# Batched matrix product in float32: loading y in 24 KB runs, transposing x on VectorE, and four 32-row tiles on TensorE

## The chip, the cores and the metric

One core of one Trainium2 chip (the experiments below ran on four chips in all, so runs are compared by their ratio to the kernel before). The metric is the device time of one execution in microseconds (us), as the median of several executions. The span of a profile is about 1.8 us shorter than the time of the same execution. A difference is called a class (faster, slower) only above 2%.

## The reference

```python
batch, dim_i, dim_j, dim_k = 32, 256, 512, 384
x: (batch, dim_i, dim_j) float32      # 16.8 MB
y: (batch, dim_j, dim_k) float32      # 25.2 MB
out = einsum('bij,bjk->bik', x, y)    # 12.6 MB, float32
```

In both kernels the matmuls take x and y with the contracted j on the partitions. y is loaded that way. x is loaded with i there, and both kernels transpose it so that j is. Both kernels multiply in float16 and accumulate in float32.

## The kernel before

The unit of work is two batches. x is loaded for four batches in one DMA, 32 partitions a batch, so each partition receives one run of 16384 B. y is loaded one batch per DMA with j spread over 128 partitions: four rows a partition, runs of 6144 B.

```python
def load_x(q):
    x_of[q] = x_pool.tile([P, R, J], F32, name="x_sb")
    keep(nc.sync.dma_start(out=x_of[q],
         in_=x[q * Q : (q + 1) * Q].rearrange("g (p r) j -> (g p) r j", r=R)))
# load(u), cut:
    y_of[u] = y_pool.tile([P, G, NJ, K], F32, name="y_sb")
    for g in range(G):
        keep(nc.sync.dma_start(out=y_of[u][:, g],
             in_=y[u * G + g].rearrange("(q t) k -> q t k", q=P)))
```

x is transposed by TensorE against an identity, in float32 into PSUM, and cast to float16 on the way out by VectorE and ScalarE in turn (128 x 512 at a time, 32 on either engine). Those two engines also cast y. A matmul contracts over 128 rows and has 64 output columns; two of them share a PSUM tile.

```python
# multiply(u), cut:
    o_ps = opsum_pool.tile([P, K], F32, name="o_ps")
    for t in range(NJ):
        for g in range(G):
            a = (u * G + g) % Q
            keep(nc.tensor.matmul(o_ps[g * M : (g + 1) * M],
                 xt_sb[:, t, e, a * PQ : (a + 1) * PQ].rearrange("c p h -> c (p h)"),
                 y_r[:, g, t], start=(t == 0), stop=(t == NJ - 1)))
```

One DMA queue carries everything. A unit's store is issued two steps after its y is cast.

## Time and profile before

| | before |
|---|---|
| median time | 136.04 us |
| span of the profile | 134.3 us |

The prediction below shows the page's main rows and what they mean. Two views that it does not show matter later. The first is the page's row of the instruction queue (queue, kind, packets, MB, share of 16 engines): packets of kind "instruction", which the page counts on the same 16 DMA engines as the data.

```profile
q8 instruction: 6, 0.10, 0.3%
```

The second is the table of stretches (stretch, us, busy us of PE, PEld, DVE, ACT and POOL with instruction counts, clock, DMA share, GB/s).

```profile
104.00:126.00 22.00, 17.58 (x156) 14.21 (x153) 11.19 (x26) 12.41 (x26) 0.00 (x0) 0.89 1.01 420
126.00:130.00 4.00, 2.40 (x30) 1.76 (x26) 1.52 (x3) 1.01 (x3) 0.00 (x0) 1.00 0.95 392
130.00:134.30 4.30, 0.00 (x0) 0.00 (x0) 0.00 (x0) 0.00 (x0) 0.00 (x0) 0.81 0.51 209
```

The last but one number is the DMA share: full until 126 us, 0.95 until 130, then the tail.

Each DMA here is spread over 16 DMA engines, and the trace records when each of them landed its part. I call the time from the first to the last of the 16 the **spread**. It is 0.6 us for the first load (landed from 8.0 to 8.6 us), 1.8 us from about 47 us on, and 2.0 us near 126 us. So some engines run behind the others, and the work that needs a DMA starts after the latest of them: the first transposes of x, for which all 16 parts had landed at 8.59, started at 8.72 us. (The records do not name the engine: "the latest" is the last of a DMA's 16 landings.)

### The profile page before, as it was taken

What the parts mean: (1) busy time and instruction counts of PE and PEld (TensorE: products, weight loads), DVE (VectorE), ACT (ScalarE), POOL (GpSimd) and SP (SyncE); (2) the same over time, 40 slices, a digit from 0 to 9 for tenths busy, and PEclk for the clock granted to TensorE, in tenths of its full rate; (3) what the DMA queues carried; (4) which work ended last, traced back from release to release, by engine and by line L of the source; (5) the groups of instructions that cost most, each with busy time, mean ns of one, the idle gap of its engine ahead of it and who ended that gap; (6) DMA issues with size and microseconds to landing.
All of it is one profiled execution on the core that took longest, in us unless ns stands there. A gap on an engine that the chain in (4) does not pass through costs nothing.

```text
span 134.3 us, 1968 instructions
## 1 busy us (share of the span) xinstructions
PE 88.5 (66%) x768; PEld 73.2 (55%) x768; DVE 56.2 (42%) x128; ACT 63.9 (48%) x129; POOL 0.7 (1%) x6
## 2 busy tenths in 40 slices
PE   0049494979299767786099771976439986597920
PEld 0049474768177666666078661864427665476810
DVE  0004717471743365711634318460363425628620
ACT  3004837662762476712744428560475336738610
POOL 2000000000000000000000000000000000000000
PEclk9999999999959999999968999999965899779997
DMA  5999999999999999999999999999999999999993
GB/s 112 415 400 450 409 417 421 456 388 421 417 448 408 409 428 421 457 394 417 413 443 436 408 417 428 442 422 402 425 423 444 426 402 427 419 427 419 417 394 158
DMA packets 8073, 54.65 MB, mean 407 GB/s; under 512 B 896, under 2 KB 896, under 8 KB 7040
## 3 DMA queue, kind: packets, MB, share of 16 engines
q1 hardware_dynamic: 8064, 54.53, 97.8%
q8 instruction: 6, 0.10, 0.3%
q14 instruction: 3, 0.02, 0.0%
HBM read 41.94 MB, written 12.58 MB: 406 GB/s over the span
## 4 chain that ended last, share of the span: by engine, by line
DMA 78%; PE 13%; ACT 4%; DVE 0%; issue 0%
DMA y_sb<-in_y_dram 40%; DMA x_sb<-in_x_dram 38%; PE o_ps L130 9%; PE t_ps L99 3%; ACT xt_sb L107 2%; ACT y_r L116 1%; ACT o_sb L143 1%; DVE o_sb L145 0%
## 5 line engine op out<-in xcount | busy, mean ns | idle before, releaser
L130 PE MATMUL o_ps<-y_r,xt_sb 128*64 128x384 f16 x512 | 52.4, 364 | 28.5 <-ACT o_sb L143 20.8
L130 PEld LDWEIGHTS <-xt_sb 128*64 128x64 f16 x512 | 39.1, 121 | 38.8 <-issue 22.4
L116 ACT CAST y_r<-y_sb 128x384 f16<-128x384 f32 x64 | 29.5, 514 | 38.7 <-DMA y_sb<-in_y_dram 38.6
L99 PE MATMUL t_ps<-identity,x_sb 128*128 128x128 f32 x256 | 36.9, 301 | 11.4 <-DMA x_sb<-in_x_dram 11.4
L99 PEld LDWEIGHTS t_ps<-identity,x_sb 128*128 128x128 f32 x256 | 34.1, 211 | 16.0 <-issue 16.0
L118 DVE CAST y_r<-y_sb 128x384 f16<-128x384 f32 x64 | 20.0, 356 | 46.7 <-DMA y_sb<-in_y_dram 46.7
L107 ACT CAST xt_sb<-t_ps 128x512 f16<-128x512 f32 x32 | 22.4, 731 | 23.6 <-PE t_ps L99 23.6
L105 DVE CAST xt_sb<-t_ps 128x512 f16<-128x512 f32 x32 | 22.6, 728 | 24.1 <-PE t_ps L99 23.8
L145 DVE COPY o_sb<-o_ps 128x384 f32<-128x384 f32 x32 | 16.3, 544 | 2.1 <-PE o_ps L130 2.1
L143 ACT COPY o_sb<-o_ps 128x384 f32<-128x384 f32 x32 | 13.9, 492 | 1.3 <-PE o_ps L130 1.3
L107 ACT ACT_TABLE_LOAD x1 | 1.3, 1283 | 0.7 <-PEq L192 0.7
masks.py:199 POOL TENSOR_SCALAR_AFFINE_SELECT identity<-identity 128x128 f32<-128x128 f32 x1 | 0.3, 294 | 0.1
masks.py:197 POOL MEMSET identity<- 128x128 f32 x1 | 0.2, 206 | 0.3 <-POOLq L192 0.3
L192 POOL MEMSET const-bfloat16-1.0<- 128x1 bf16 x1 | 0.1, 102 | 0.0
L192 POOL MEMSET const-uint8-127<- 128x1 uint8 x1 | 0.1, 102 | 0.0
L192 POOL MEMSET const-float32-0.0<- 128x1 f32 x1 | 0.1, 99 | 0.2 <-issue 0.2
L192 POOL MEMSET const-float32-1.0<- 128x1 f32 x1 | 0.1, 99 | 0.0
## 6 DMA issues: line engine op xcount, KB each, us to landing
y_sb<-in_y_dram SPq DMA_DIRECT2D x32, 768.0 KB, 17.9
x_sb<-in_x_dram SPq DMA_DIRECT2D x8, 2048.0 KB, 20.8
out_dram<-o_sb SPq DMA_DIRECT2D x16, 768.0 KB, 17.8
```

Of the source, the lines that this page charges most:

```text
L99: nc.tensor.transpose(t_ps[:, f, h], x_sb[:, h * NE + e + f, t::NJ], identity)
L105: keep(nc.vector.tensor_copy(dst, t_ps))
L107: keep(nc.scalar.copy(dst, t_ps))
L116: keep(nc.scalar.copy(yr_of[u][:, g, t], y_sb[:, g, t]))
L118: keep(nc.vector.tensor_copy(yr_of[u][:, g, t], y_sb[:, g, t]))
L130: nc.tensor.matmul(o_ps[g * M : (g + 1) * M], xt_sb[:, t, e, a * PQ : (a + 1) * PQ].rearrange("c p h -> c (p h)"), y_r[:, g, t], start=(t ...
L143: keep(nc.scalar.copy(o_of[u][:, e], ps_of[u][e]))
L145: keep(nc.vector.tensor_copy(o_of[u][:, e], ps_of[u][e]))
L192: nc = _bacc.Bacc("TRN2", target_bir_lowering=False, num_devices=1)
```

## The change

The intent: fewer and longer DMA packets for y, no transposes on TensorE (and no casts on ScalarE), four small matmuls at once. The unit becomes a group of four batches, 32 partitions a batch for both x and y, so a partition's y run is 24576 B. x is cast to float16 and its 4-byte words (pairs of float16) are transposed in 32 x 32 blocks by VectorE. Matmuls contract over 32 rows with 128 output columns, and a group fills all eight buffers of the PSUM pool ("banks" in the prediction). ScalarE copies them out in blocks of 64 partitions, VectorE half of those of the last group. Stores are issued a group's load later (DEFER = 3).

```diff
-Q = 4; G = 2; LAG = 4
+Q = 4; WIDE = 32; NARROW = 64; DEFER = 3
...
+    def load(n):                       # x as before, then y:
+        y_of[n] = y_pool.tile([P, T, K], F32, name="y_sb")
+        src = y[n * Q : (n + 1) * Q].rearrange("g (q t) k -> (g q) t k", t=T)
+        parts = 4 if n == N - 1 else 1
+        for a in range(parts): ...     # one DMA for each part
...
+    def transpose_x(n):
+        x_r = xr_pool.tile([P, R, J], MM_DT, name="x_r")
+        keep(nc.vector.tensor_copy(x_r, x_of.pop(n)))                    # L83
+        words = x_r.bitcast(F32)
+        src = words.rearrange("p (b h e) (q t) -> p b e t h q", b=2, e=NE, t=TW)
+        dst = xt_of[n].rearrange("p e t (h s b) -> p b e t h s", s=PQ, b=2)
+        for e in range(NE):
+            for b in range(2):
+                keep(nc.vector.transpose(dst[:, b, e], src[:, b, e]))    # L96
...
+    def multiply(n):                   # for each of 4 pieces a of y:
+            keep(nc.vector.tensor_copy(y_r[:, a : a + step], y_sb[:, a : a + step]))  # L107
+            for e in range(NE):
+                for t in range(a, a + step):
+                    for g in range(Q):
+                        s = slice(g * PQ, (g + 1) * PQ)
+                        keep(nc.tensor.matmul(ps_of[n][e][g],            # L113
+                             xt[s, e, t // 2, :, t % 2], y_r[s, t],
+                             start=(t == 0), stop=(t == T - 1)))
...
+    for n in range(2):
+        load(n)
+    for n in range(N):
+        transpose_x(n)
+        multiply(n)
+        collect(n)                     # copies: L139 ScalarE, L137 VectorE
+        if n + 2 < N:
+            load(n + 2)
+        if n + 2 - DEFER >= 0 and n + 2 < N:
+            store(n + 2 - DEFER)
+    for n in range(N - DEFER, N):
+        store(n)
```

(Lines reflowed and cut; all of the old load, transpose, round_y, multiply, collect and store is removed. `pieces(n)` is 4 and `width(n)` is NARROW for every group.)

More of the change, by code (lines that the diff above doesn't have):

```diff
@@ L15 @@
 Q = 4
-G = 2
-LAG = 4
+WIDE = 32
+NARROW = 64
+DEFER = 3
 @with_exitstack
@@ L32 @@
     _, _, K = y.shape
-    M = P // G
-    NE = I // M
-    NJ = J // P
     PQ = P // Q
     R = I // PQ
-    H = R // NE
-    U = B // G
-    const_pool = ctx.enter_context(tc.tile_pool(name="const", bufs=1))
-    x_pool = ctx.enter_context(tc.tile_pool(name="x_pool", bufs=3))
-    y_pool = ctx.enter_context(tc.tile_pool(name="y_pool", bufs=5))
+    T = J // PQ
+    TW = T // 2
+    NE = I // P
+    N = B // Q
+    x_pool = ctx.enter_context(tc.tile_pool(name="x_pool", bufs=2))
+    y_pool = ctx.enter_context(tc.tile_pool(name="y_pool", bufs=2))
@@ L49 @@
+    xr_pool = ctx.enter_context(tc.tile_pool(name="xr_pool", bufs=1))
+    xt_pool = ctx.enter_context(tc.tile_pool(name="xt_pool", bufs=2))
     yr_pool = ctx.enter_context(tc.tile_pool(name="yr_pool", bufs=2))
-    xt_pool = ctx.enter_context(tc.tile_pool(name="xt_pool", bufs=2))
-    o_pool = ctx.enter_context(tc.tile_pool(name="o_pool", bufs=5))
-    tpsum_pool = ctx.enter_context(tc.tile_pool(name="tpsum", bufs=4, space=bass.MemoryType.PSUM))
-    opsum_pool = ctx.enter_context(tc.tile_pool(name="opsum", bufs=4, space=bass.MemoryType.PSUM))
+    o_pool = ctx.enter_context(tc.tile_pool(name="o_pool", bufs=DEFER + 2))
@@ L56, with width, pieces @@
+    psum_pool = ctx.enter_context(
+        tc.tile_pool(name="psum", bufs=2 * Q, space=bass.MemoryType.PSUM)
+    )
     keep = tc.keep_in_program_order
-    identity = const_pool.tile([P, P], F32)
-    make_identity(nc, identity)
-    x_of, y_of, yr_of, xt_of, ps_of, o_of = {}, {}, {}, {}, {}, {}
-    def load_x(q):
-        x_of[q] = x_pool.tile([P, R, J], F32, name="x_sb")
+    x_of, y_of, xt_of, yr_of, ps_of, o_of = {}, {}, {}, {}, {}, {}
+    def width(n):
+        return NARROW
+    def pieces(n):
+        return 4
@@ L65, in load_x @@
+    def load(n):
+        x_of[n] = x_pool.tile([P, R, J], F32, name="x_sb")
         keep(
             nc.sync.dma_start(
-                out=x_of[q],
-                in_=x[q * Q : (q + 1) * Q].rearrange("g (p r) j -> (g p) r j", r=R),
-            )
-        )
-    def load(u):
-        if u == 0:
-            load_x(0)
-        if (u + 1) * G % Q == 0 and u + 1 < U:
-            load_x((u + 1) * G // Q)
-        y_of[u] = y_pool.tile([P, G, NJ, K], F32, name="y_sb")
-        for g in range(G):
+                out=x_of[n],
+                in_=x[n * Q : (n + 1) * Q].rearrange("g (p r) j -> (g p) r j", r=R),
+            )
+        )
+        y_of[n] = y_pool.tile([P, T, K], F32, name="y_sb")
+        src = y[n * Q : (n + 1) * Q].rearrange("g (q t) k -> (g q) t k", t=T)
+        parts = 4 if n == N - 1 else 1
+        for a in range(parts):
+            s = slice(a * T // parts, (a + 1) * T // parts)
+            keep(nc.sync.dma_start(out=y_of[n][:, s], in_=src[:, s]))
@@ new lines, in transpose_x @@
+    def transpose_x(n):
+        x_r = xr_pool.tile([P, R, J], MM_DT, name="x_r")
+        keep(nc.vector.tensor_copy(x_r, x_of.pop(n)))
+        xt_of[n] = xt_pool.tile([P, NE, TW, P], F32, name="xt_sb")
+        words = x_r.bitcast(F32)
+        if width(n) == WIDE:
+            src = words.rearrange("p (h e) (q t) -> p e t h q", e=NE, t=TW)
+            dst = xt_of[n].rearrange("p e t (h s) -> p e t h s", s=PQ)
+            for e in range(NE):
+                keep(nc.vector.transpose(dst[:, e], src[:, e]))
+        else:
+            src = words.rearrange("p (b h e) (q t) -> p b e t h q", b=2, e=NE, t=TW)
[3 more added lines that the diff above has]
+                    keep(nc.vector.transpose(dst[:, b, e], src[:, b, e]))
@@ new lines, in multiply @@
+    def multiply(n):
+        xt = xt_of.pop(n).bitcast(MM_DT).rearrange("p e t (m c) -> p e t m c", c=2)
+        y_sb = y_of.pop(n)
+        y_r = yr_pool.tile([P, T, K], MM_DT, name="y_r")
+        ps_of[n] = [
+            [psum_pool.tile([P, K], F32, name="o_ps") for _ in range(Q)] for _ in range(NE)
+        ]
+        step = T // pieces(n)
+        for a in range(0, T, step):
+            keep(nc.vector.tensor_copy(y_r[:, a : a + step], y_sb[:, a : a + step]))
+            for e in range(NE):
+                for t in range(a, a + step):
+                    for g in range(Q):
+                        s = slice(g * PQ, (g + 1) * PQ)
+                        keep(
+                            nc.tensor.matmul(
+                                ps_of[n][e][g],
+                                xt[s, e, t // 2, :, t % 2],
+                                y_r[s, t],
+                                start=(t == 0),
+                                stop=(t == T - 1),
+                            )
+                        )
@@ new lines, in collect @@
+    def collect(n):
+        w = width(n)
+        per = P // w
+        o_of[n] = o_pool.tile([P, R, K], F32, name="o_sb")
+        o = o_of[n].rearrange("p (u f) k -> p u f k", u=Q // per)
+        for u in range(Q // per):
+            for e in range(NE):
+                for v in range(per):
+                    g = u * per + v
+                    ps = ps_of[n][e][g]
+                    on_vector = n == N - 1 and g % 2 == 1
+                    for h in range(per):
+                        src = ps[h * w : (h + 1) * w]
+                        dst = o[v * w : (v + 1) * w, u, h * NE + e]
+                        if on_vector:
+                            keep(nc.vector.tensor_copy(dst, src))
+                        else:
+                            keep(nc.scalar.copy(dst, src))
+        del ps_of[n]
@@ L80, in load, with store @@
+    def store(n):
+        w = width(n)
+        per = P // w
+        o = o_of.pop(n).rearrange("p (u f) k -> p u f k", u=Q // per)
+        for u in range(Q // per):
+            b = n * Q + u * per
             keep(
                 nc.sync.dma_start(
-                    out=y_of[u][:, g],
-                    in_=y[u * G + g].rearrange("(q t) k -> q t k", q=P),
-                )
-            )
-    def transpose(q, half):
-        x_sb = x_of[q]
-        if half == 0:
-            xt_of[q] = xt_pool.tile([P, NJ, NE, Q * PQ, H], MM_DT, name="xt_sb")
-        n = 0
-        for t in range(half * NJ // 2, (half + 1) * NJ // 2):
-            for e in range(0, NE, 2):
-                t_ps = tpsum_pool.tile([P, 2, H, Q * PQ], F32, name="t_ps")
-                for f in range(2):
-                    for h in range(H):
-                        keep(
-                            nc.tensor.transpose(
-                                t_ps[:, f, h], x_sb[:, h * NE + e + f, t::NJ], identity
-                            )
-                        )
-                dst = xt_of[q][:, t, e : e + 2].rearrange("c f p h -> c f h p")
-                if n % 2 == 0:
-                    keep(nc.vector.tensor_copy(dst, t_ps))
-                else:
-                    keep(nc.scalar.copy(dst, t_ps))
-                n += 1
@@ L110, in round_y @@
-    def round_y(u):
-        y_sb = y_of.pop(u)
-        yr_of[u] = yr_pool.tile([P, G, NJ, K], MM_DT, name="y_r")
-        for g in range(G):
-            for t in range(NJ):
-                if t % 2 == 0:
-                    keep(nc.scalar.copy(yr_of[u][:, g, t], y_sb[:, g, t]))
-                else:
-                    keep(nc.vector.tensor_copy(yr_of[u][:, g, t], y_sb[:, g, t]))
-    def multiply(u):
-        xt_sb, y_r = xt_of[u * G // Q], yr_of.pop(u)
-        ps_of[u] = []
-        for e in range(NE):
-            o_ps = opsum_pool.tile([P, K], F32, name="o_ps")
-            ps_of[u].append(o_ps)
-            for t in range(NJ):
-                for g in range(G):
-                    a = (u * G + g) % Q
-                    keep(
-                        nc.tensor.matmul(
-                            o_ps[g * M : (g + 1) * M],
-                            xt_sb[:, t, e, a * PQ : (a + 1) * PQ].rearrange("c p h -> c (p h)"),
-                            y_r[:, g, t],
-                            start=(t == 0),
-                            stop=(t == NJ - 1),
-                        )
-                    )
@@ L139, in collect @@
-    def collect(u):
-        o_of[u] = o_pool.tile([P, NE, K], F32, name="o_sb")
-        for e in range(NE):
-            if e % 2 == 0:
-                keep(nc.scalar.copy(o_of[u][:, e], ps_of[u][e]))
-            else:
-                keep(nc.vector.tensor_copy(o_of[u][:, e], ps_of[u][e]))
-        del ps_of[u]
-    def store(u):
-        keep(
-            nc.sync.dma_start(
-                out=out[u * G : (u + 1) * G].rearrange("g (m e) k -> (g m) e k", e=NE),
-                in_=o_of.pop(u),
-            )
-        )
@@ L157 @@
-    ahead = LAG - 2
-    for u in range(ahead):
-        load(u)
-    for s in range(U + 2):
-        if s + ahead < U:
-            load(s + ahead)
-        if s == 0:
-            transpose(0, 0)
-            transpose(0, 1)
-        if s >= 2:
-            collect(s - 2)
-        if 1 <= s <= U:
-            multiply(s - 1)
-        if s < U:
-            round_y(s)
-        for half in range(2):
-            q = (s + 1 - half) * G // Q
-            if (s + 1 - half) * G % Q == 0 and 0 < q < B // Q:
-                transpose(q, half)
-        if s >= 2:
-            store(s - 2)
+                    out=out[b : b + per].rearrange("g (s f) k -> (g s) f k", s=w),
@@ L181 @@
+                    in_=o[:, u],
+                )
+            )
+    for n in range(2):
[10 more added lines that the diff above has]
+        store(n)
 _INS = ['x', 'y']
```

## The prediction

> **What bounds the kernel now.** I read the page from the top: busy shares, the 40 slices, the DMA queue, the chain that ended last, then the groups of instructions. After that I read the timeline of TensorE and of the last 30 us, and the trace's records of single DMA packets. First the page.
>
> ```profile
> span 134.3 us, 1968 instructions
> PE 88.5 (66%) x768; PEld 73.2 (55%) x768; DVE 56.2 (42%) x128; ACT 63.9 (48%) x129; POOL 0.7 (1%) x6
> ...
> PEclk9999999999959999999968999999965899779997
> DMA  5999999999999999999999999999999999999993
> ...
> DMA packets 8073, 54.65 MB, mean 407 GB/s; under 512 B 896, under 2 KB 896, under 8 KB 7040
> ...
> q1 hardware_dynamic: 8064, 54.53, 97.8%
> ...
> DMA 78%; PE 13%; ACT 4%; DVE 0%; issue 0%
> ```
>
> No compute engine passes 66%. The DMA row is at 9 from the second slice to the last but one, the queue's packets fill 97.8% of 16 engines' time, and the chain is 78% DMA. So the kernel is bound by the time its DMA packets take. The packet records split that time: 1024 packets of 16384 B (x, one per partition and load), median 611 ns; 6144 of 6144 B (4096 of y, 2048 of the output), median 234 ns, mean 235.8; 896 semaphore writes of 9 ns (56 DMAs x 16 engines). Per engine that is 40.3 + 90.6 + 0.5 = 131.4 us. The data packets run from 1.78 to 132.93 us, so there is almost no hole. The x sum holds about 1.1 us of slow first packets (26 of them over 700 ns, up to 1996). The only hole worth a name is at the end: in the last 4 us the engines lose about 1 us, part of it because the last store is issued at 129.1 us, after the last copy out of PSUM. The span ends 1.3 us after the last packet, and the timed median is 136.04 - 134.3 = 1.8 us over the profiled span.
>
> Next, the engines that the change reworks, in the table of groups and two pieces of TensorE's timeline (start, length, what):
>
> ```profile
> L130 PE MATMUL o_ps<-y_r,xt_sb 128*64 128x384 f16 x512 | 52.4, 364 | 28.5 <-ACT o_sb L143 20.8
> ...
> L99 PE MATMUL t_ps<-identity,x_sb 128*128 128x128 f32 x256 | 36.9, 301 | 11.4 <-DMA x_sb<-in_x_dram 11.4
> ...
> L118 DVE CAST y_r<-y_sb 128x384 f16<-128x384 f32 x64 | 20.0, 356 | 46.7 <-DMA y_sb<-in_y_dram 46.7
> ...
> L143 ACT COPY o_sb<-o_ps 128x384 f32<-128x384 f32 x32 | 13.9, 492 | 1.3 <-PE o_ps L130 1.3
> ```
>
> ```profile
> 107.94 2.79 PE L130 MATMUL o_ps<-y_r,xt_sb 128*64 128x384 f16 x32 [0.87 <-ACT xt_sb L107]
> ...
> 115.54 4.47 PE L130 MATMUL o_ps<-y_r,xt_sb 128*64 128x384 f16 x32 [2.69 <-ACT o_sb L143]
> ```
>
> In the first burst 32 matmuls start (2.79 - 0.33) / 31 = 79.5 ns apart, where one takes 326 ns from start to end: two column tiles run at once, 159 ns each. The second burst is the same work after an idle stretch of 2.69 us, and takes 1.7 us longer: that is the PEclk row's 5s, a clock record of 3.4 us at half rate. Two ScalarE copies in a row take 0.87 us in the timeline, so one costs 0.39 us more behind another (0.48 alone).
>
> [...]
>
> **The change part by part.**
>
> DMA. x and the output keep their runs (16384 and 6144 B). y goes from 4096 packets of 6144 B to 7 groups of 128 partitions at 24576 B = 896, and the last group in four parts, 512 of 6144 B. From the two medians a packet costs (611 - 234) / (16384 - 6144) = 0.0368 ns a byte and 8 ns fixed, so 24576 B take 913 ns, with the usual excess 915. That such a run stays one packet is my assumption; all shorter ones do. Per engine: x 40.3; y 896 x 0.915 / 16 = 51.2 and 512 x 0.2358 / 16 = 7.5; output 2048 x 0.2358 / 16 = 30.2; semaphores 35 DMAs x 0.009 = 0.3. Sum 129.6, against 131.4: **1.8 us less**. If the last stores are ready in time, up to 0.3 us of the hole at the end goes too.
>
> TensorE loses the 256 fp32 transposes (36.9 us) and has 1024 matmuls of 32 rows x 128 columns in place of 512: if four row tiles run at once, 159 / 4 = 40 ns apart, 128 x 0.040 = 5.1 us a group of four batches. I use 40 to 55 ns, as the weight loads of 128 columns may not all hide, and add 1.7 us for the clock: 6.8 to 8.7 us.
>
> VectorE per group: [...] Sum 8.4 (11) us of the roughly 16 us that a group's DMA takes (8 packets per engine of x, 8 of y, 16 of output: 4.9 + 7.3 + 3.8). It lies beside the transfers.
>
> ScalarE loses all casts (51.9 us) and takes all copies out of PSUM but half of the last group's: 16 a group of 64 partitions. The free size is unchanged, so I take the same 0.39 to 0.43 us: 6.3 to 6.9 us a group.
>
> What is new is a loop. One group fills all 8 PSUM banks, so the next group's first matmuls must wait until the twelfth of the 16 copies has freed the fourth bank. Copies of the first half of the banks start some 16 matmuls before the burst ends (0.7 us). Loop = matmuls - 0.7 + 12 x 0.41 + about 0.3 for handing over = 6.8 + 4.5 = 11.3, to 8.7 + 4.5 = 13.2 us. What it may be: y0 lands near 16 us (x0 lands at 8.6 in this trace, plus 7.3), then y lands every 12.2 us three times (no stores yet) and every 16 us four times, the last near 117. The loop falls behind in the first part and catches up in the second. DMA then still has three groups' deferred stores (11.2 us) while the last group computes: matmuls, then 4 copies on each of two engines per half. For the last stores to be ready when the queue gets to them (near 126.5), the last burst must begin by about 116.5, so the loop may last (116.5 - 17) / 7 = 14.2 us. At 11.3 to 13.2 it is hidden, and so is its cost; loads are issued a group or more ahead (x waits only for its cast, y for its casts), so the queue should not run dry.
>
> Sum: 136.04 - 1.8 - 0.15 = **134.1 us**.
>
> **Rivals.** (a) Row tiles do not overlap well, or weight loads go one after another. For: 64-column loads last 110 ns here, and fp32 transposes with 128-column loads come 16 in 2.19 us on the timeline, (2.19 - 0.28) / 15 = 127 ns apart. Against: the two column tiles reach 79.5 ns, with loads longer than that hidden. If 107 ns apart (127 scaled down as fp16 needs less, a guess), a burst is 13.7 + 1.7 and the loop near 19.5 us: 17 + 7 x 19.5 + 15 + 4 + 4 = about 176 us. (b) The loop is a little over 14.2: the PEclk row shows half clock after idle stretches under 3 us, and here the idle stretch is over 4; with twice the penalty at 55 ns it is 15, last burst at 122, and the end 5 us late: 138. Each further us of loop costs 7. (c) The transfer is hidden or unchanged anyway, that is, the 24 KB packet brings no gain over four of 6 KB: then 136. (d) The 24 KB packets gain more, or the end closes wholly (1 us): 133.2.
>
> **Range and chances.** The DMA gain is a difference of measured durations, so the centre is firm if the loop hides. About one in five goes to (a) and a bad (b), over 138.8; to pass 133.3 the gain would have to be 2.7 us, against 1.8 to 2.1 expected, which I give one in eight. The rest is within 2%. The range runs from 133.0 to 139.5, with room upward for a loop of about 15 us.
>
> **What would show it.** Right: the queue's packets at 1408 of y in place of 4096, 24 KB ones near 913 ns; DMA at 9 to the end; the chain still DMA; matmul bursts under 9 us a group[...]. Wrong: DMA slices below 9 in the middle, a chain of PE and ACT, and idle TensorE released by ACT copies with bursts 14 us long (a), or clock rows at 5 throughout (b). The prediction falls if a group's loop measures over 14.2 us, or a 24 KB run is split into small packets.

VectorE's sum per group came to 8.4 us, and the 11 in brackets is the same sum with the transposes doubled, in case their strided source is slow. No term of the 134.1 us comes from it, as VectorE was taken to lie beside the transfers. What the trace of before does show of these engines: VectorE's cast of 128 x 384 from SBUF took 356 ns and its copy of as many elements from PSUM 544; a weight load took 121 ns in the mean for 64 float16 columns (median 110) and 211 ns for 128 float32 columns. That four matmuls of 32 rows run at once was an assumption: before has two at once, 79.5 ns apart in the mean. The 55 ns and the 107 ns between matmuls are allowance and guess.

## The result, and the profile after

The time was **136.78 us** (136.75 to 137.25, four executions) against 136.05 (135.92 to 136.08, four executions) in the same rounds: a ratio of 1.0064, interval 1.0048 to 1.008. Ratios here are the mean time of one kernel's runs over that of the other's of the same rounds, so not quite the ratio of the medians quoted. The class is "same", for which the prediction's chances leave about two in three, and the time lies inside the predicted range. But the prediction was a gain of 1.9 us, and there is a loss of 0.7 us, clear of the scatter: 2.6 to 2.7 us are to be explained. The profiled execution was the slowest of the four, 137.25 us.

The page after, its rows that answer to those of before:

```profile
span 135.5 us, 2381 instructions
...
PE 64.2 (47%) x1024; PEld 33.7 (25%) x1024; DVE 83.6 (62%) x80; ACT 58.0 (43%) x121; POOL 0.2 (0%) x4
...
PEclk9999999975797579757975698556985698556985
DMA  4999999999999998999999999999999999999765
...
DMA packets 5050, 54.68 MB, mean 404 GB/s; under 512 B 560, under 2 KB 560, under 8 KB 3120
...
q1 hardware_dynamic: 5040, 54.53, 96.2%
q8 instruction: 8, 0.13, 0.4%
...
DMA 76%; DVE 13%; PE 5%; SPq 1%; issue 1%; DVEq 1%
```

Of the y packets of 6144 B, 3584 have become 896 of 24576 B as planned, the chain is still DMA, and no engine passes 62%. Two things differ from the forecast. The DMA row no longer holds 9 to the end: it falls to 7, 6, 5. And the chain has 13% of VectorE in it, where before had none. There are also 8 instruction packets in place of 6.

The groups of instructions after (busy us, mean ns of one, idle before them and what ended it):

```profile
L113 PE MATMUL o_ps<-y_r,xt_sb 32*128 32x384 f16 x1024 | 64.2, 415 | 62.9 <-DVE y_r L107 61.0
L139 ACT COPY o_sb<-o_ps 64x384 f32<-64x384 f32 x120 | 56.7, 473 | 71.6 <-PE o_ps L113 45.5
...
L83 DVE CAST x_r<-x_sb 128x4096 f16<-128x4096 f32 x8 | 18.4, 2294 | 33.3 <-DMA x_sb<-in_x_dram 33.3
L107 DVE CAST y_r<-y_sb 128x1536 f16<-128x1536 f32 x32 | 28.5, 953 | 8.6 <-DMA y_sb<-in_y_dram 8.6
L96 DVE STREAM_TRANSPOSE xt_sb<-x_r 128x512 f32<-128x512 f32 x32 | 32.4, 1072 | 0.7
```

An x cast took 2.29 us, a y cast 0.95 and a transpose 1.07. For a group the timeline below has 2.29 + 4.03 + 3.52 = 9.8 us, where the forecast had a sum of 8.4.

The timeline after from 111 us, the last group (start, length, what):

```profile
111.82 2.29 DVE L83 CAST x_r<-x_sb 128x4096 f16<-128x4096 f32 x1 [5.09 <-DMA x_sb<-in_x_dram]
114.22 4.03 DVE L96 STREAM_TRANSPOSE xt_sb<-x_r 128x512 f32<-128x512 f32 x4
118.18 3.52 DVE L107 CAST y_r<-y_sb 128x1536 f16<-128x1536 f32 x4
...
119.15 7.91 PE L113 MATMUL o_ps<-y_r,xt_sb 32*128 32x384 f16 x128 [8.09 <-DVE y_r L107]
...
126.48 3.88 ACT L139 COPY o_sb<-o_ps 64x384 f32<-64x384 f32 x8 [8.18 <-issue]
126.54 4.56 DVE L137 COPY o_sb<-o_ps 64x384 f32<-64x384 f32 x8 [4.84 <-PE o_ps L113]
```

Read down, this is a staircase: the last x is complete at 111.7, VectorE needs until 119.1 for cast, transposes and the first y piece, TensorE until 127.06, the copies until 131.1, and the second half of the store can only be issued then, at 131.2. The prediction needed the burst to start by 116.5. The table of stretches shows what that leaves:

```profile
126.00:130.00 4.00, 1.06 (x28) 0.41 (x20) 3.36 (x7) 3.42 (x8) 0.00 (x0) 1.00 0.59 242
130.00:135.50 5.50, 0.00 (x0) 0.00 (x0) 1.09 (x2) 0.37 (x1) 0.00 (x0) 0.61 0.64 260
```

The DMA share from 126 to 130 us is 0.59 where it was 0.95: there is nothing left to send.

That looks like the whole answer, but the landing records say no. In the same trace the last DMAs landed, first to last of the 16 engines, at 124.9 to 128.5, 126.7 to 130.4, 132.0 to 132.2 and 134.2 to 134.4 us. The fast engines did stand idle between 126.7 and 132. The latest engine went 128.5, 130.4, 132.2, 134.4, in steps of 1.8 to 2.2, almost without a hole. Had the last stores been ready early, I estimate from these steps that it would still have ended near 130.4 + 2 x 1.85 = 134.1. So two causes end the run at nearly the same time, and each hides the other: a late last store, and engines that lag 3.7 us (2.0 before). Taking the packet times themselves, the mean per engine did fall, from 131.37 to 130.29 us. The lag ate it. A small part lies after the last landing: the span ends 1.06 us after it, where before it ended 0.84 us after it. In the trace SyncE checks its last semaphores one after another, some 0.065 us each. The semaphore that lands last is the last of its list before; after, four more checks follow it.

### The profile page after: what moved, and what is told of

Read it like the earlier page. It is cut to its first block, busy times and chain, and to the rows that moved or that the text cites. A ratio compares the mean times of both kernels' runs of the same rounds, so it can differ in the third digit from the quotient of the medians. Undisturbed runs are those within 1.5% of the kernel's fastest.

```text
span 135.5 us, 2381 instructions
## 1 busy us (share of the span) xinstructions
PE 64.2 (47%) x1024; PEld 33.7 (25%) x1024; DVE 83.6 (62%) x80; ACT 58.0 (43%) x121; POOL 0.2 (0%) x4
## 4 chain that ended last, share of the span: by engine, by line
DMA 76%; DVE 13%; PE 5%; SPq 1%; issue 1%; DVEq 1%
DMA x_sb<-in_x_dram 76%; DVE x_r L83 7%; PE o_ps L113 5%; DVE xt_sb L96 3%; DVE o_sb L137 3%; DVE y_r L107 1%; DVEq L192 0%; SPq L77 0%; SPq L67 0%; DVEq L83 0%; DVEq L137 0%; DVEq L96 0%
## 5 line engine op out<-in xcount | busy, mean ns | idle before, releaser
L113 PE MATMUL o_ps<-y_r,xt_sb 32*128 32x384 f16 x1024 | 64.2, 415 | 62.9 <-DVE y_r L107 61.0
L139 ACT COPY o_sb<-o_ps 64x384 f32<-64x384 f32 x120 | 56.7, 473 | 71.6 <-PE o_ps L113 45.5
L113 PEld LDWEIGHTS <-xt_sb 32*128 32x128 f16 x1024 | 33.7, 116 | 93.0 <-DVE y_r L107 46.6
L83 DVE CAST x_r<-x_sb 128x4096 f16<-128x4096 f32 x8 | 18.4, 2294 | 33.3 <-DMA x_sb<-in_x_dram 33.3
L107 DVE CAST y_r<-y_sb 128x1536 f16<-128x1536 f32 x32 | 28.5, 953 | 8.6 <-DMA y_sb<-in_y_dram 8.6
L96 DVE STREAM_TRANSPOSE xt_sb<-x_r 128x512 f32<-128x512 f32 x32 | 32.4, 1072 | 0.7
L137 DVE COPY o_sb<-o_ps 64x384 f32<-64x384 f32 x8 | 4.4, 556 | 5.0 <-PE o_ps L113 4.8
```

The costliest lines, as they stand in the source:

```text
L83: keep(nc.vector.tensor_copy(x_r, x_of.pop(n)))
L96: keep(nc.vector.transpose(dst[:, b, e], src[:, b, e]))
L107: keep(nc.vector.tensor_copy(y_r[:, a : a + step], y_sb[:, a : a + step]))
L113: nc.tensor.matmul(ps_of[n][e][g], xt[s, e, t // 2, :, t % 2], y_r[s, t], start=(t == 0), stop=(t == T - 1),)
L137: keep(nc.vector.tensor_copy(dst, src))
L139: keep(nc.scalar.copy(dst, src))
```

## The experiments

Two theories were on the table at first. H (hole): the staircase of the last group delays the last stores. L (lag): some of the 16 engines fall further behind than before, and the latest sets the end. A third, P (packets): the 24 KB packets bring no gain by themselves. Fifteen runs (of thirteen kernels, as `repeat` is the changed kernel and d4b is defer4 again) were made. In the second and later lots the base is DEFER = 4, which closes the hole and leaves L and P (and changes one thing more, see defer4). The measurements, with the landing records of the profiled execution of each:

| run | median us | ratio to before (95%) | mean packet time per engine | spread near 126 us | last store landed, first to last engine | instruction packets |
|---|---|---|---|---|---|---|
| before | 136.05 | | 131.37 | 2.0 | 132.2 to 133.4 | 6 |
| after | 136.78 | 1.0064 (1.0048 to 1.008) | 130.29 | 3.7 | 134.2 to 134.4 | 8 |
| repeat | 137.27 | 1.0057 (1.0031 to 1.0083) | 130.48 | 4.5 | 133.3 to 134.7 | 8 |
| defer4 | 136.62 | 1.0021 (0.9991 to 1.0052) | 129.98 | 3.0 | 130.3 to 133.2 | 8 |
| y6k | 137.09 | 1.0061 (1.0038 to 1.0084) | 131.65 | 3.2 | 134.8 to 135.0 | 8 |
| xahead | 140.54 | 1.0316 (1.0292 to 1.034) | 130.00 | 2.8 | 137.6 to 137.8 | 8 |
| d4b | 136.37 | 1.0009 (0.9988 to 1.003) | 129.95 | 3.4 | 130.0 to 133.4 | 8 |
| d4_y6k | 136.27 | 1.0008 (0.9988 to 1.0027) | 131.70 | 2.0 | 131.7 to 133.6 | 8 |
| d4_fetch | 137.45 | 1.008 (1.0061 to 1.01) | 130.35 | 4.4 | 130.4 to 134.8 | 15 |
| d4_dense | 136.08 | 0.9983 (0.9962 to 1.0004) | 129.93 | 3.2 | 130.2 to 133.4 | 8 |
| d4_stx | 136.55 | 1.0027 (1.0006 to 1.0049) | 130.68 | 2.8 | 132.2 to 133.6 | 8 |
| d4_half | 136.67 | 1.0029 (1.0013 to 1.0045) | 130.60 | 2.5 | 130.9 to 133.4 | 8 |
| d4_12k | 136.44 | 1.0027 (0.9997 to 1.0056) | 130.54 | 2.8 | 130.7 to 133.5 | 8 |
| d4_fewmm | 135.94 | 0.9994 (0.9974 to 1.0013) | 130.07 | 2.8 | 130.3 to 133.1 | 1 |
| d4_fewmm_y6k | 137.21 | 1.0089 (1.0062 to 1.0116) | 132.00 | 3.2 | 131.4 to 134.6 | 1 |
| d4_pair | 135.60 | 0.995 (0.9932 to 0.9968) | 129.59 | 2.6 | 130.2 to 132.8 | 8 |
| d4_two | 135.55 | 0.9947 (0.9932 to 0.9962) | 129.51 | 2.5 | 130.0 to 132.5 | 8 |

The medians of before in the five lots were 136.25, 136.25, 136.18, 136.03 and 136.25. All results are correct but those of d4_dense, d4_fewmm and d4_fewmm_y6k.

### repeat: the changed kernel once more

No edit.

> The changed kernel again, unaltered, as a control. Theory A (the end): the last stores are issued too late because the last group's chain, x cast 2.3 us + four transposes 4.0 + first y cast 0.95 + matmul burst 7.9 + copies 4.6, hangs on the landing of the last x; the DMA engines again lose about 1.7 us on average near 127 to 130 us. Theory B (slow packets): the cluster of 24 KB packets of 1.0 to 2.2 us around 50 us and 84 us in the first profile (1.1 us per engine over all) comes back. Time 136.8 either way; if B is a property of the packets, their mean is again near 933 ns, otherwise near 915.

Measured: 137.27 (136.61 to 137.52), ratio 1.0057. The loss is real. The executions fall in two heaps, 136.6 to 136.7 and 137.1 to 137.5, and the profiled one (137.52) is of the upper. In it the first engine landed the last store at 133.3 and the latest at 134.7, with a spread of 4.5 before it and steps of 1.8 to 1.9 on the latest engine: in this execution the lag alone set the end. Clusters of slow 24 KB packets sit where they sat in the first trace (below), so they are no accident of one execution.

### defer4: one more group's store held back

```diff
-DEFER = 3
+DEFER = 4
```

> Four groups of stores are held back in place of three, so the last x and y land about 3.7 us earlier and the queue has 15 us of stores for the time of the last group's work. Nothing else changes. Theory A: the hole near 127 to 130 us closes, and the time falls by 0.5 to 1.7 us, to 135.1 to 136.3. Theory B, or the slowest DMA engine sets the end (it idled only 0.3 us in the first profile): at most 0.3 us less, 136.5.

Measured: 136.62 against 137.27 for the changed kernel in the same rounds; the intervals overlap (0.9991 to 1.0052, 1.0031 to 1.0083). The hole is gone; its DMA row, from the page:

```profile
DMA  5999999999999999999999999999999999999991
```

The last store was issued at 126.6, not 131.2, and the last x landed at 107.4, not 111.7: with one store less ahead of it in the queue the last group starts 4.3 us earlier. So the hole was real and is closed, and still only 0.65 us came of it, and no gain over before. The six executions fall in two heaps here too (136.01 to 136.22 and 137.01 to 137.13); d4b, the same kernel, has 136.14 to 136.72. The edit also changes the order of the queue: it now goes back from stores to loads three times, not four, which matters below, so not even the 0.65 us is the hole's alone. H is part of the answer at most; the spread is still 3.0.

### y6k: y in 6 KB runs again, all else as changed

```diff
-        parts = 4 if n == N - 1 else 1
+        parts = 4
```

> Every y group is loaded in four parts with runs of 6144 B, as the last group already is; all else stays. If a 24 KB run is worth what the packet medians say (912 ns against 4 x 234), DMA work grows by 56 x 24 ns = 1.3 us per engine plus 21 more semaphore writes of 9 ns = 0.2, and the time goes to about 138.2. If the 24 KB packets lose their gain again in slow packets (theory B), the time stays within 0.3 us of 136.8 or falls.

Measured: 137.09, ratio 1.0061, the same as the changed kernel. Read alone this would say P: the long packets are worth nothing. But the mean packet time rose to 131.65 from 130.48 in `repeat`, and the last store landed within 0.2 us on all engines (134.8 to 135.0) after a hole: the staircase set this end, whatever the packets cost. With the hole in place, this comparison cannot tell.

### xahead: x loaded, cast and transposed a group ahead

```diff
-    for n in range(2):
-        load(n)
+    load_x(0); load_x(1); load_y(0)
+    transpose_x(0)
+    load_x(2); load_y(1)
     for n in range(N):
-        transpose_x(n)
+        if n + 1 < N:
+            transpose_x(n + 1)
         multiply(n)
         collect(n)
+        if n + 3 < N:
+            load_x(n + 3)
         if n + 2 < N:
-            load(n + 2)
+            load_y(n + 2)
```

> x is loaded, cast and transposed one group ahead of y, so the last group's x work (6.3 us on VectorE) is done before the last y lands. Same transfers in another order. Theory A: the last burst starts at the twelfth copy of the group before or at the first part of the last y, about 2.7 us earlier than 119.2, the last stores are issued about 2.7 us earlier, and the time falls by 0.5 to 1.7 us. Theory B: no change over 0.3 us.

Measured: 140.54, 3.2% slower: a clear miss. The edit takes x's 6.3 us off the staircase, and puts the loads of the last two y close together (y6 after x7). The timeline of this run shows what came in their place:

```profile
108.79 7.97 PE L115 MATMUL o_ps<-y_r,xt_sb 32*128 32x384 f16 x128 [8.64 <-DVE y_r L109]
...
116.17 7.83 ACT L141 COPY o_sb<-o_ps 64x384 f32<-64x384 f32 x16 [8.78 <-issue]
...
123.07 0.47 PE L115 MATMUL o_ps<-y_r,xt_sb 32*128 32x384 f16 x1 [0.51 <-ACT o_sb L141]
...
124.05 6.51 PE L115 MATMUL o_ps<-y_r,xt_sb 32*128 32x384 f16 x109 [0.51 <-ACT o_sb L141]
...
129.84 3.88 ACT L141 COPY o_sb<-o_ps 64x384 f32<-64x384 f32 x8 [5.84 <-issue]
```

y7's first piece was cast at 113.3, but the bulk of the last burst starts at 124.05: single matmuls drip, about 0.98 us apart, as ScalarE frees one buffer after another. From burst to burst this loop takes 124.05 - 108.79 = 15.3 us, where the prediction had 11.3 to 13.2. Matmuls go in program order over all eight buffers (single ones at 117.18, 118.16, 119.14 us and so on, each released by a ScalarE copy), so the bulk waits for the last of the 16 copies, not for the twelfth, and the copies come 7.83 / 16 = 0.49 us apart, not 0.41. The loop is the 15 us of rival (b), over the limit of 14.2 us, but not for (b)'s reason, a doubled clock penalty: the burst before it took 7.97 us, inside the forecast of 6.8 to 8.7. In the changed kernel the loop is only just hidden, because there the last x arrives late anyway: the copies ended at 118.3 us and the last burst began at 119.15.

### d4b and d4_y6k: packets of 24 KB and 6 KB with the hole closed

d4b is defer4 again; d4_y6k has both edits, DEFER = 4 and parts = 4.

> The kernel with four groups of stores held back, again, as the base of this set. Expected as in the first job: 136.0 to 137.1, DMA busy without a hole to the end, the landing spread between the first and the last of the 16 DMA engines near 3 us at the end.

> Four groups of stores held back and y in 6144 B runs throughout. With the hole at the end closed, the DMA term stands alone. If the mean DMA work sets the time, it rises by the whole packet gain, 1.3 us less the slow 24 KB packets (0.4 to 0.8): 0.5 to 1.5 us over the base. If the slowest engine sets it and the slow 24 KB packets fall on that engine, the time stays within 0.4 us of the base.

Measured: 136.37 and 136.27. There is no hole in either now, the mean packet time differs by 131.70 - 129.95 = 1.75 us, and the times do not differ. The landing records of the last store say why: the first engine landed it at 130.0 with 24 KB and at 131.7 with 6 KB, 1.7 us apart, as the packets promise. The latest engine landed it at 133.4 and 133.6. The gain exists on the fast engines, and the end belongs to the latest one. The 0.2 us that is left goes after the last landing (1.06 us from there to the end of the span with 24 KB, 0.82 with 6 KB). This is L, and P falls.

The sorted lags of the 16 engines behind the first show how it grows. With 24 KB near 124.5 us eight engines were within 1.31 us and five at 2.8 to 3.4; with 6 KB near 126.1 seven were within 0.83 and nine at 1.6 to 2.0. The steps have a source that the trace shows: instruction packets. One is 16384 B on queue q8 and took 0.90 to 1.10 us in the profiles of before and after; in 12 of their 14 cases a data packet that starts as it ends took 0.36 to 0.55 us over the median of its size. Together that is about 1.5 us, and one more of the 16 landings is about that late from then on (in before, after its first such packet, the latest landing went from 0.62 to 1.55 us behind the first). In d4_y6k the spread jumps from 0.8 to 2.0 us at the first such packet (24.4 us). In the kernel before, two engines are late at 43.3 us (by 1.58 and 1.78 us), after its first two. In d4b the late ones were 1.1 to 2.0 us behind at 56.6 us, after three such packets and before any store, and 2.6 to 3.2 us at 95.6: with 24 KB packets the late engines lose more on the way. Both kernels have eight instruction packets, and so d4_y6k's spread of 2.0 is that of before, which has six. In d4_y6k each further such packet made one more engine late and left the spread where it was.

### d4_fetch: more instruction packets

```diff
+        if n > 0:                      # in multiply, on DEFER = 4
+            old_xt, old_y = last
+            for _ in range(128):
+                keep(nc.tensor.matmul(ps_of[n][0][0][:, :16],
+                     old_xt[0:PQ, 0, 0, :, 0], old_y[0:PQ, 0, :16],
+                     start=True, stop=True))
```

The dummy matmuls write what the real ones overwrite; the result stays correct.

> Four groups of stores held back, and 128 more small matmuls of 16 columns ahead of the burst of each group but the first, on data that is there already, overwritten by the real ones: 1792 more TensorE instructions, so about 7 more 16 KB instruction fetches, each of which takes about 1.5 us of one DMA engine. If those fetches are what spreads the DMA engines and costs the change its gain, the landing spread grows from 3 to 4.5 us or more and the time by 0.5 to 2 us. If not, the time stays within 0.3 us of the base, or falls a little[...].

The page's row of that queue:

```profile
q8 instruction: 15, 0.25, 0.7%
```

Measured: 137.45, so 1.1 us more than d4b in the same rounds, intervals apart (1.0061 to 1.01, 0.9988 to 1.003). Seven more instruction packets; the mean packet time rose by 0.40, the spread by 1.0 to 4.4, the last landing by 1.3 to 134.8, while the last four DMAs still landed 1.8 to 1.9 apart on the first engine: no new hole. Not a byte of data was added. The dummies also change TensorE's hours, so this is a strong hint rather than a pure test. (The real matmuls took 404 ns in the mean, 396 in d4b.)

### d4_dense: what makes the transposes slow

Four forms of the transpose, one for each of the four calls of a group.

```diff
+            dense = words.rearrange("p (b h e) (t q) -> p b e t h q", b=2, e=NE, t=TW)
+            flat = xt_of[n].rearrange("p e t (b h s) -> p b e t h s", s=PQ, b=2)
+            keep(nc.vector.transpose(dst[:, 0, 0], src[:, 0, 0]))     # L96, as it was
+            keep(nc.vector.transpose(dst[:, 1, 0], dense[:, 1, 0]))   # L97, source dense
+            keep(nc.vector.transpose(flat[:, 0, 1], src[:, 0, 1]))    # L98, target dense
+            keep(nc.vector.transpose(flat[:, 1, 1], dense[:, 1, 1]))  # L99, both
```

> Wrong result on purpose. Of the four transposes of each group one is as it was, one reads its words densely (step 1 in place of 8), one writes densely (step 1 in place of 2), one does both. If the strides make a 512-word transpose cost 1.07 us[...], the dense ones fall[...]; if it is the four-byte element, all four stay at 1.07. If the transposes are what slows 24 KB packets in clusters (they coincide), shorter or denser transposes thin the clusters out. Time: the base, or up to 0.5 us less.

The table of groups of this run:

```profile
L96 DVE STREAM_TRANSPOSE xt_sb<-x_r 128x512 f32<-128x512 f32 x8 | 8.8, 1106 | 0.7
L98 DVE STREAM_TRANSPOSE xt_sb<-x_r 128x512 f32<-128x512 f32 x8 | 8.5, 1057 | 0.0
L99 DVE STREAM_TRANSPOSE xt_sb<-x_r 128x512 f32<-128x512 f32 x8 | 5.4, 672 | 0.0
L97 DVE STREAM_TRANSPOSE xt_sb<-x_r 128x512 f32<-128x512 f32 x8 | 5.4, 670 | 0.0
```

Measured: the source's step of eight words costs the time (1106 and 1057 ns strided, 672 and 670 dense); the target's step of two words costs little or nothing (1106 against 1057 ns with the strided source, 670 against 672 with the dense one). The time of the whole was 136.08 (0.9983, 0.9962 to 1.0004), an interval that overlaps d4b's (0.9988 to 1.003), for 0.8 us less of VectorE a group. With DEFER = 4 the transposes are not what sets the end.

### d4_stx, d4_half, d4_12k: where the slow packets are

The other part of the lag is in the packets themselves. The records of single packets in the changed kernel have a median of 912 ns for 24576 B (forecast 913) but a mean of 933: most are at the median, and some take 1.0 to 2.2 us. They come in clusters, at 49 to 51, 83 to 85 and 98 to 101 us, at the same places in `repeat`; with DEFER = 4 the first is a group later (61 to 64 us). The first cluster is in the y load that the first store follows. Above the median they add up to 1.2 us per engine after (0.71 in d4b). So I suspected the changes from reads to writes and back. d4_stx puts the stores between the load of x and that of y; d4_half uses 24 KB only for the groups that are loaded before stores begin; d4_12k uses two parts of 12 KB.

```diff
# d4_stx, on DEFER = 4
         if n + 2 < N:
-            load(n + 2)
+            load_x(n + 2)
         if n + 2 - DEFER >= 0 and n + 2 < N:
             store(n + 2 - DEFER)
+        if n + 2 < N:
+            load_y(n + 2)
# d4_half, on DEFER = 4
-        parts = 4 if n == N - 1 else 1
+        parts = 4 if n >= DEFER else 1
# d4_12k, on DEFER = 4
-        parts = 4 if n == N - 1 else 1
+        parts = 4 if n == N - 1 else 2
```

> Four groups of stores held back, and each group's stores stand between the x load and the y load in the queue in place of after the y load. Same packets. So far 24 KB packets were slow (1.0 to 2.2 us) in clusters only in y loads that a store follows in the queue (the first cluster came one group later when stores were held back one group longer). Theory E, it is the store right behind y that slows y's last packets: the clusters go, the excess of the 24 KB packets falls from 0.7 to under 0.3 us an engine, the landing spread from 3.3 to about 2, and the time by 0.7 to 1.4 us, to 135.0 to 135.7. Theory F, the stores anywhere beside the y reads, or something of 24 KB reads itself: clusters and time stay (136.3).

> Four groups of stores held back; y in 24 KB runs for the first four groups, which saw no slow clusters, and in 6144 B runs for the other four. Both theories: spread near 2, mean work about 0.7 to 0.9 us an engine under the all-6144 kernel's 131.7, and so 135.4 to 135.7. If the spread is not due to the slow 24 KB packets, it stays near 3 and the time near 136.3.

> Four groups of stores held back; y in two parts with runs of 12288 B. From the medians a 12 KB packet costs 460 ns, so the mean work without slow packets is 0.45 us over the 24 KB kernel's. If slow clusters come with packets over some size, there may be none here: spread 2, time 135.4 to 135.8. If they come with stores whatever the size, in proportion to the bytes: near 136.3.

Measured: 136.55, 136.67 and 136.44, none better than before, and their intervals overlap, so none of the three settles anything by its time. Their packets tell more. In d4_stx the excess of the 24 KB packets fell from 0.71 to 0.30 us per engine, and that of the 16 KB packets of x (counted after 10 us, as the first packets are slow in every run) rose from 0.13 to 0.88: the slow ones moved to the load that now lies next to the stores. In d4_half the 24 KB packets had only 0.12 left, as none of them lies near a store; the gain of the long packets was halved with them (mean 130.60). Its spread fell to 2.5, where near 2 was forecast, and its time did not fall at all, a miss: the mean rose by 0.65 over d4b's, and in the profiled execution the span ran 1.6 us past the last landing, where other 24 KB runs have 1.0 to 1.1. Slow 24 KB reads are thus not the whole of the lag. In d4_12k the 12 KB packets had clusters too, at 79 to 81 and 95 to 97 us. So slow reads go with the stores' neighbourhood, and not with 24 KB as such. What in the chip makes them slow, no run here shows.

### d4_fewmm and d4_fewmm_y6k: almost no instruction packets

Only the first and the last of 16 steps of the contraction are multiplied, 128 matmuls in place of 1024, so that TensorE's program is short; the result is wrong.

```diff
-                for t in range(a, a + step):
+                for t in (t for t in range(a, a + step) if t in (0, T - 1)):
```

d4_fewmm_y6k has parts = 4 besides; both have DEFER = 4.

> Wrong result on purpose: four groups of stores held back, y in 24 KB runs, and only the first and the last of the 16 contraction steps multiplied, so 128 matmuls in place of 1024 and at most one TensorE instruction fetch in place of eight. All transfers and all VectorE and ScalarE work stay. If the fetches make some DMA engines late, and the late engines set the end, the landing spread falls from 3.3 to about 1 to 1.5 us and the time by 1.5 to 2.5 us, to 133.9 to 134.9. If the spread comes from the 24 KB reads themselves, it stays near 3 and the time near 136.3.

> Wrong result on purpose: the same with y in 6144 B runs. Without the fetches the packet gain should stand in the time: 1.3 to 1.8 us more than the 24 KB kernel of this set, with a spread near 1 in both. If the 24 KB gain is lost for another reason, the two times agree within 0.4 us.

The page's row of the instruction queue in d4_fewmm:

```profile
q8 instruction: 1, 0.02, 0.0%
```

Measured: 135.94 and 137.21. Between the two, 24 KB is worth 0.95% or 1.27 us, in the same rounds with intervals apart: here the long packets do pay, and about what they should. But against d4b the short program brought only 0.4 us by the medians, 0.2 by the ratios, where I expected much more: a miss. The spread stayed at 0.9 us (d4_fewmm) and 1.1 (d4_fewmm_y6k) until the stores began, near 64 us, which is what L says of instruction packets. After that it grew all the same, to 2.8 and 3.2, and this time it was the 16 KB reads of x that were slow (excess 0.78 and 0.80, against 0.13 and 0.25 with the full program). d4_fewmm_y6k is even about 1 us slower than d4_y6k, although its program is shorter. So instruction packets are one source of the lag; with them gone, slow reads came in their place. Why x is hit here and y there stays open.

### d4_pair and d4_two: fewer changes between reads and writes

If slow reads come with each turn from writing back to reading, fewer turns should leave fewer of them. d4_pair stores two groups at a time at two points; d4_two stores two groups once, before the last load, and the other six at the end.

```diff
# d4_pair, on DEFER = 4
         if n + 2 < N:
             load(n + 2)
-        if n + 2 - DEFER >= 0 and n + 2 < N:
-            store(n + 2 - DEFER)
-    for n in range(N - DEFER, N):
+        if n in (3, 5):
+            store(n - 3)
+            store(n - 2)
+    for n in range(4, N):
         store(n)
# d4_two, on DEFER = 4
+        if n == 5:
+            store(0)
+            store(1)
         if n + 2 < N:
             load(n + 2)
-        if n + 2 - DEFER >= 0 and n + 2 < N:
-            store(n + 2 - DEFER)
-    for n in range(N - DEFER, N):
+    for n in range(2, N):
         store(n)
```

> Six output buffers as with four groups held back, but stores go two groups at a time, after the loads of groups 5 and 7, and the last four groups at the end: two changes from reading to writing and back in place of four. If slow reads come at each such change, the packets' excess falls by about a half (0.7 to about 0.35 us an engine), the spread to about 2.5, and the time to 135.6 to 136.0. If they come with the bytes written, no change: 136.3.

> Only the first two groups are stored on the way, ahead of the last group's loads, and six groups at the end: one change from reading to writing and back. If slow reads come at each change, the excess of the 24 KB packets is under 0.3 us an engine, the spread near 2 (the instruction fetches), and the time 135.0 to 135.6, under both kernels. The risk: reads alone fill the queue until group 5, groups arrive every 12.2 us against a loop of burst and copies of 13.6 to 15.3 us, so the last burst may start late and leave a hole at the end: then 136 to 138.

The rows of DMA in d4_two:

```profile
DMA  5999999999999999999999999999999999999992
...
q1 hardware_dynamic: 5040, 54.53, 97.0%
q8 instruction: 8, 0.13, 0.4%
```

Measured: **135.60 and 135.55**, ratios 0.995 and 0.9947, both below before and, with intervals apart, below d4b (0.9988 at the least). The excess of the 24 KB packets fell from 0.71 to 0.25 and 0.22 us per engine, the mean packet time to 129.59 and 129.51, which is the 129.6 of the prediction; the spread fell from 3.4 to 2.6 and 2.5, and the last landing from 133.4 to 132.8 and 132.5. The two expectations count the turns wrongly. Read from the edits and from the issue times, the queue of d4b goes back from stores to loads three times, with three groups' stores ahead of some load; d4_pair and d4_two go back once each, with two groups' stores, since d4_pair's second pair comes after the last load. So the two runs differ little, as their results do. The excess fits the turns: 1.20 and 1.07 us with four (after, repeat), 0.66 and 0.71 with three (defer4, d4b), 0.25 and 0.22 with one. But the stored bytes among the loads fell too, so which of the two it is was not tested apart. d4_two is correct, and the fastest version found: 0.5% below the kernel before and 1.2% below the changed one by the ratios to before (1.0064 / 0.9947). The eight instruction packets remain, and the spread stays above the 2.0 of before. Whether 6 KB packets would be as fast in this order was not tried.

## Why the prediction was right or wrong

**Bound.** That DMA packet time bounds both kernels was right: the chain is 76% DMA after and no engine passes 62%.

**The DMA step: "Sum 129.6, against 131.4: 1.8 us less".** The mechanism was right and its unit too (912 ns measured for 913), and the packet stayed whole, 896 of them. This is nevertheless the step that failed first, in two ways. The mean came to 130.29: the 24 KB term was made from the median with an excess of 2 or 3 ns a packet, and the slow ones near stores, up to 2.16 us, made it 21 ns, 1.2 us per engine in place of 0.2 (x's excess fell by 0.3). And the sum is a mean over 16 engines, while the end belongs to the latest one. The prediction has no term for the spread; it was 2.0 us before and 3.7 and 4.5 after in the two profiled executions. In d4b against d4_y6k it cancels 1.4 of 1.75 us of packet time. Instruction packets (more with d4_fetch) and slow reads (fewer with d4_two) are two sources that the runs show; the step from 6 instruction packets to 8 is not enough, as d4_y6k has 8 and a spread of 2.0. That they are all, no run shows: d4_fewmm had nearly none of the first and still 2.8 us.

The number of instruction packets could have been estimated ahead from the page of before: TensorE has 768 matmuls and 768 weight loads there and the queue 6 packets, 1536 / 6 = 256 instructions a packet. At that rate the 2048 of after make 8; in d4_fetch 896 dummies with their loads make 7 more, 15; in d4_fewmm 256 make 1. The pages show exactly 8, 15 and 1.

**"If the last stores are ready in time, up to 0.3 us of the hole at the end goes too."** They were not: the last went out at 131.2, two microseconds later than before's.

**VectorE: "It lies beside the transfers."** Wrong for the last group. The x cast took 2.29 us, the four y casts 3.5 to 3.6, and the transposes 1.07 us each, 4.03 for the four, which overlap a little: 9.8 us, between the sum of 8.4 and the 11 that the prediction has in brackets but does not use at the end. For the other groups no run shows a cost. For the last, 6.3 us from x's landing to the end of the transposes stand before the burst, and the prediction's loop has no such term: it times the end by PSUM alone.

**"the last burst must begin by about 116.5 ... At 11.3 to 13.2 it is hidden, and so is its cost".** The burst began at 119.15, and not because of PSUM. Bursts averaged (119.15 - 17.09) / 7 = 14.6 us in the changed kernel, paced by loads; the PSUM loop proper is 15.3 us where xahead lays it bare. Of its terms the burst was right (7.9 us, the first 5.1 at half clock, in 6.8 to 8.7), the copies are 0.49 us apart (one of 64 partitions took 473 ns, one of 128 had taken 492 before), and the bulk waits for 16 of them. Rival (b) has a loop of 15 us, though from the clock and not from the copies, and an end five microseconds late; the loop came true only in xahead. In the changed kernel the missed start opened the hole, but the hole and the lag ran side by side: closing it (with one turn fewer) gave 0.65 us of the 2.7, with overlapping intervals.

**TensorE and rival (a).** Right, and (a) is out: four matmuls start within 11 ns of one another every 0.16 us at full clock, 40 ns apart in the mean, and every 0.32 at half clock (the last burst of after), and a weight load of 128 float16 columns took 116 ns in the mean, against 211 for 128 float32 columns before. (By the prediction's own formula (a)'s loop is 19.9 us, not 19.5, and (b)'s end five microseconds after 134.1 is 139, not 138; neither changes the argument.)

**Rival (c)**, "the transfer is hidden or unchanged anyway ... then 136", was nearest in number. Its reason was not right: the packets do gain (1.7 us on the first engine), and the lag hides it.

**The account.** Forecast 1.9 us faster, found 0.7 slower. As the hole and the lag overlap, the 2.7 us cannot be split into shares that add up. Holding a fourth group back gave 0.65; fewer turns gave a further 0.8 (1.0009 to 0.9947 is 0.62% of 136.25); about 1.2 us of the 2.7 is left (0.9947 x 136.04 = 135.3, against 134.1). In the profiled execution of d4_two the spread is still 0.5 us above that of before, and the stretch after the last landing 0.2 us longer. The rest stays open: what slows large reads beside stores, why engines that are late stay late with 24 KB, and why x is hit with a short program.

## What to carry to other kernels

When a DMA queue is always full, sum the packets by the latest of the 16 engines and not by their mean: look at how far apart the parts of one transfer land, and ask what each change does to that (here they were 2.0 us apart before and 3.7 after, and a lower mean, 130.29 us for 131.37, came with a longer time). Longer packets showed in the time in one pair of runs (d4_fewmm, 1.27 us) and not in another (d4b, nothing), so a sum of packet times alone does not say what they are worth. The order of loads and stores in the queue was worth 0.6% with the same packets, and a longer TensorE program came with DMA packets of its own (15 in place of 8 in d4_fetch, with 1.1 us more time). And work out the last group's path from its landing to its last store by itself, since what is hidden in every other group is bare there.
